# A decoder layer on one core: the first block of a seven-product matmul evicted in another order, its difference operands made later

## The chip, the cores and the metric

The kernel runs on one core of a Trainium2 chip. The metric is the device time of one execution in microseconds (us). Engines are named as in the profile: PE is TensorE (matmuls; PEld its weight loads), DVE is VectorE, ACT is ScalarE, POOL is GpSimd, SP is SyncE, which issues most of the DMAs.

## The reference, cut to what matters

One layer of a decoder trunk, for one batch of 512 tokens with model width 1024, all in float32:

```
h  = RMSNorm(x);  z = h @ W_in
A  = retention(z);  Bt = dilated windowed attention(z)
x  = x + (sig(g_A) * (A @ W_A) + sig(g_B) * (Bt @ W_B)) @ W_o
x  = x + relu(RMSNorm(x) @ W_up)^2 @ W_down          # W_down is 4096 x 1024
x  = x + sig(RMSNorm(x) @ W_pg) * (p @ W_pp)
```

The change touches the two steps `... @ W_o` and `... @ W_down`, and the very start of the kernel.

## The kernel before

Every large matmul is done in three: each operand is split into a high part (rounded to the matmul's float32r type) and a low part (the rest), and high x high, high x low and low x high are added up in PSUM (`mm3`, lines 246 to 251). So each weight block must be split on its way. A weight block of 128 x 1024 per partition row set is called a unit. `make_plan` lists all units in the order in which they are used. `fetch` (line 187) issues a unit's load from SP into one of six `raw` buffers, for some units with a second, adding DMA from POOL (L202) into the same buffer. `ahead` (line 205) runs the split of a unit: ACT rounds `raw` into `whi` (L237), DVE subtracts into `wlo` (L238), each in one of four buffers. `units(n)` (line 217) is called by a gemm for its next units; it has all units up to `AHEAD` further ones split, so AHEAD sets how early in the program the splits stand.

**The seven-product matmul.** `@ W_o` and each 1024-row part of `@ W_down` is a 2 x 2 block matmul in Strassen's way: seven products of combined blocks in place of eight. `seven_gemm` (line 1001) does it, five times in the kernel: first for W_o (in `tail`, line 1099), then four times for W_down (line 1149). The left operands were combined and split before (`seven_left`). The right operands are sums or differences of weight blocks. `plan_seven` (line 164) plans 14 units for it, two halves of the inner dimension for each product. Numbered from 0, in the order of use: units 0 to 5 are products 4, 3, 5 for the first half and again for the second; 6 and 7 are product 2; 8 and 9 product 1; 10 and 11 product 7; 12 and 13 product 6. Units 8 and 9 load nothing: each is a difference of blocks that are already in `raw` buffers, those of units 6 and 2, and of units 7 and 5. `ahead` makes both differences in place on DVE (L215) right behind the split of unit 7. They free the raw buffers of units 2 and 5 for later loads.

One product with one half is 12 matmuls of 512 columns on PE, six for each of two token blocks p. Product 4 gathers in two banks of PSUM, 3 in two more, 5 in two; 2 is added later on top of 4's banks, 7 on 5's and 6 on 3's; product 1 has two banks of its own. Hence bank 4 must be copied out (`m4`, ACT, L1040) before product 2 starts. The results are added to the residual x by `acc` on DVE (L1026). The copies and the first accumulations stand behind the sixth product step, product 5 with half 1.

**What follows each finished part.** `done` calls `ready`, which puts a transpose of the finished part of x in a list with a lag in ticks (`gain_T`, line 358); a product step ticks once behind the matmuls of each p, and a tick issues one ripe item (`tick`, line 115). The item (`split_T`, line 318) is four PE transposes (L325), then the split of their result out of PSUM, on ACT (L338, `h2h` or `h3h`) and DVE (L339, `h2l` or `h3l`). For tokens 0 to 255, columns 512 to 1023, the lag is one tick, and the PSUM banks are those of product 1, which starts two product steps later. `ready` exists for the first of the five matmuls (it feeds the MLP) and for the last (it feeds the gate); the three between have none.

**What sets the order.** The tile framework's planner orders the instructions of each engine. For the first matmul and the last, the kernel puts ACT and DVE under `manual_schedule` (lines 1097 and 1146), so that these two engines keep the written order there; PE and the DMA queues don't. The three matmuls between are left to the planner. AHEAD is set to 3 for the first and the last; `seven_gemm` sets 2 before product 7, and so the three between run with 2.

**The start.** `setup` clears a tile `warm` (L406), has ACT touch one element of it (L407) and runs seven bfloat16 matmuls on it (L410) while the first data arrive. Those matmuls read 512 bfloat16 columns, which are the first 256 of the tile's 512 float32 columns.

Of the kernel before, what the change touches and what calls it, by code (L numbers as in the profile page):

```python
# [13 lines left out]
AF = mybir.ActivationFunctionType  # L14
ALU = mybir.AluOpType
# [57 lines left out]
def R(ap):  # L73
    return ap.bitcast(F32R)


class Block:
# [86 lines left out]
    def plan_seven(self, w, r0):  # L164


        q = lambda i, j, u: w[r0 + 512 * i + 256 * u : r0 + 512 * i + 256 * (u + 1), 512 * j : 512 * (j + 1)]
        n = len(self.plan)
        for u in range(2):
            self.plan.append(((q(1, 0, u), q(0, 0, u)), None))  # L170
            self.plan.append(((q(0, 1, u), q(1, 1, u)), None))
            self.plan.append((q(1, 1, u), None))
        for u in range(2):
            self.plan.append((q(0, 0, u), None))
        self.differences[n + 7] = [(n + 6 + u, n + 2 + 3 * u) for u in range(2)]
        for u in range(2):
            self.plan.append(((None, n + 6 + u, n + 2 + 3 * u), None))
        for u in range(2):
            self.plan.append(((q(1, 0, u), q(1, 1, u)), None))
        for u in range(2):  # L180
            self.plan.append(((q(0, 0, u), q(0, 1, u)), None))
# [23 lines left out]
    def ahead(self, n):  # L205
        while len(self.loaded) < min(len(self.plan), self.used + n):
            i = len(self.loaded)
            self.fetch(i + 1)
            raw, g0 = self.raws[i]
            src = self.plan[i][0]  # L210
            if isinstance(src, tuple) and src[0] is None:
                g0 = None
            self.loaded.append(self.split_unit(raw, g0))
            for v, w in self.differences.get(i, ()):
                self.nc.vector.tensor_tensor(self.raws[v][0], self.raws[v][0], self.raws[w][0], op=ALU.subtract)  # L215

    def units(self, n):
        self.ahead(n + (0 if self.pinned else self.AHEAD))
# [158 lines left out]
    def setup(self):  # L377
        nc, a = self.nc, self.a
        self.gcol = self.const.tile([P, 48], F32, name="gcol")
        xr = [self.big("xr") for _ in range(2)]  # L380
        self.x_cols = [xr[k // 4][:, k % 4] for k in range(KD)]
        nc.scalar.dma_start(self.gcol, a["vec_cols"])
        for u in range(KD // 2):
            src, _ = self.plan[u]
            raw = self.wraw.tile([P, 1024], F32, tag="raw", name=self.nm("raw")).rearrange("p (k n) -> p k n", k=2)
            for k in range(2):
                c = slice((2 * u + k) * P, (2 * u + k + 1) * P)
                first = u == 0 and k == 0
                x = lambda i: nc.sync.dma_start(self.x_cols[2 * u + k][:, i], a["x_cols"][c, i])
                x(slice(0, 256) if first else slice(0, S))  # L390
                nc.sync.dma_start(raw[:, k], src[k * P : (k + 1) * P])
                if first:
                    x(slice(256, S))
            self.raws.append((raw, None))
        self.load_tables()
        self.fetch(6)
        self.x_tiles = []
        xb = [self.big("x") for _ in range(2)]
        for t in range(NT):
            v = xb[t // 2].rearrange("p (t c) n -> p t (c n)", t=2)[:, t % 2]  # L400
            nc.sync.dma_start(v, a["x"][0, t * P : (t + 1) * P])
            self.x_tiles.append(v)
        self.ident = self.const.tile([P, P], F32, name="ident")
        make_identity(nc, self.ident)
        warm = self.tmp("warm")
        nc.vector.memset(warm, 0.0)  # L406
        nc.scalar.activation(warm[:, 500:501], warm[:, 501:502], AF.Copy)  # L407
        wb, wps = warm.bitcast(mybir.dt.bfloat16), self.bank("warm")
        for _ in range(WARM):
            nc.tensor.matmul(wps, wb[:, :P], wb[:, :512], start=True, stop=True)  # L410
        self.mhalf = self.const.tile([P, H], F32, name="mhalf")
        nc.gpsimd.memset(self.mhalf, -0.5)
# [588 lines left out]
    def seven_gemm(self, U, xs, f, ready):  # L1001


        nc = self.nc
        LEFT = {1: 3, 2: 4, 3: 0, 4: 6, 5: 1, 6: 5, 7: 2}
        banks = {}

        def product(m, bank, u, first, last):
            (wh, wl), = self.units(1)
            for p in range(2):  # L1010
                if first and m != 1:
                    banks[bank, p] = self.gbank() if m in (3, 4) else self.bank("pb")
                ps = banks[bank, p]
                for k in range(2):
                    kk = 2 * u + k
                    c = slice(LEFT[m] * 256 + p * P, LEFT[m] * 256 + (p + 1) * P)
                    sh, sl = (R(U[i][kk].rearrange("p a b -> p (a b)")[:, c]) for i in range(2))
                    self.mm3(ps, sh, sl, wh[:, k], wl[:, k], first and k == 0, last and k == 1, m != bank)
                self.tick()

        X = lambda i, j, p: xs[2 * i + p][:, 512 * j : 512 * (j + 1)]

        def acc(i, j, p, v, sign=0):
            t, x = 2 * i + p, X(i, j, p)
            c = sign * NT + t
            nc.vector.scalar_tensor_tensor(x, v, f[:, c : c + 1], x, op0=ALU.mult, op1=ALU.add)  # L1026

        def done(i, j, p):
            if ready is not None:
                ready(2 * i + p, j, banks.get((1, p)))  # L1030

        for u in range(2):
            for m in (4, 3, 5):
                product(m, m, u, u == 0, u == 1)
        m4 = []
        for p in range(2):
            banks[1, p] = self.bank("pb")
        for p in range(2):
            t = self.tmp("m4")
            nc.scalar.activation(t, banks[4, p], AF.Copy)  # L1040
            m4.append(t)
            acc(0, 1, p, banks[3, p])
            acc(0, 1, p, banks[5, p], 1)
            done(0, 1, p)
        for u in range(2):
            product(2, 4, u, False, u == 1)
        for p in range(2):
            acc(1, 0, p, banks[4, p])
            done(1, 0, p)
            acc(1, 1, p, banks[4, p], 1)  # L1050
        for u in range(2):
            product(1, 1, u, u == 0, u == 1)
        for p in range(2):
            nc.vector.tensor_tensor(m4[p], m4[p], banks[1, p], op=ALU.add)
            acc(0, 0, p, m4[p])
            acc(1, 1, p, m4[p])
        self.AHEAD = 2
        for u in range(2):
            product(7, 5, u, False, u == 1)
        for p in range(2):  # L1060
            acc(0, 0, p, banks[5, p])
            done(0, 0, p)
        for u in range(2):
            product(6, 3, u, False, u == 1)
        for p in range(2):
            acc(1, 1, p, banks[3, p])
            done(1, 1, p)
# [165 lines left out]
```

## Time and profile before

| | us |
|---|---|
| runs | 993.36, 993.45, 993.88 (median 993.45) |
| the profiled execution | 993.55 |
| its span, first to last instruction | 991.8 |
| PE busy / DVE / ACT / POOL | 984.9 / 648.8 / 462.1 / 98.1 |
| L215 on DVE, ten instructions, each | 1.22 |
| L237 on ACT, 128x1024, each | 1.06 |
| L238 on DVE, 128x1024, each | 1.22 |

The first of the five matmuls runs on PE from 558.2 us of the span, the last from 900.2. A row of a timeline is: start, length, engine, line, operation, output and inputs by the program's names, shapes, count; in brackets the idle time of the engine before it and what ended it. Rows of the chain of waits are start, length and what was running. Lengths of matmul rows are modelled and overlap the next matmul; their starts are what counts. A row of busy times by window is: the window, its length, busy time, count, the clock granted to PE, the busy share of the DMA engines, GB/s.

### The profile page before, as it was taken

Reading aid. Unit: us, or ns where it says so; the run is one execution under the profiler, and the core shown is the slowest. Engines: PE = TensorE matmul, PEld = TensorE weight load, DVE = VectorE, ACT = ScalarE, POOL = GpSimd, SP = SyncE. Lnnn points to the kernel's source line nnn. Section 1 sums busy time; section 2 is a strip of 40 time slices with the busy share of each in tenths; the row PEclk is TensorE's granted clock in tenths of the full one; section 3 lists DMA queues with packets and bytes.
Section 4 is the critical chain, followed back from the end, with each engine's and each line's share of the span. In section 5 each row is a group of like instructions: output and inputs, shape, how many; then the busy total and the mean of one; then the engine's idle time right before and its main releaser. Section 6 shows DMA issues by size and latency. Waiting matters only on the chain.

```text
span 991.8 us, 12456 instructions
## 1 busy us (share of the span) xinstructions
PE 984.9 (99%) x4588; PEld 826.7 (83%) x4588; DVE 648.8 (65%) x1015; ACT 462.1 (47%) x939; POOL 98.1 (10%) x98
## 2 busy tenths in 40 slices
PE   9999999999999999999999999999999999999998
PEld 6888899889888888888888888888888888888886
DVE  7858675774869345454733796678667769767953
ACT  6635344433334334243423448664563565465451
POOL 0310120220000010001002000100101001000000
PEclk9999999999999999999999999999999999999999
DMA  9723122333234322222446486758749767875911
GB/s 333 262 85 87 44 85 85 113 98 98 83 109 153 124 63 76 96 65 86 162 135 156 137 218 201 185 141 221 184 132 226 187 159 170 228 174 128 298 54 54
DMA packets 90910, 141.16 MB, mean 142 GB/s; under 512 B 6320, under 2 KB 40672, under 8 KB 90848
## 3 DMA queue, kind: packets, MB, share of 16 engines
q1 hardware_dynamic: 79824, 119.36, 37.3%
q0 software_dynamic: 10880, 20.97, 12.6%
q8 instruction: 36, 0.59, 0.2%
q14 instruction: 26, 0.21, 0.1%
q10 hardware_dynamic: 144, 0.02, 0.0%
HBM read 136.10 MB, written 4.24 MB: 141 GB/s over the span
## 4 chain that ended last, share of the span: by engine, by line
PE 97%; DVE 1%; ACT 1%; DMA 1%; SPq 0%; issue 0%; ACTq 0%; DVEq 0%
PE pg L249 27%; PE pg L251 27%; PE pg L250 27%; PE pb L251 3%; PE pb L250 3%; PE pb L249 3%; PE po L699 1%; PE ph L555 1%; PE pt L325 1%; PE sc L676 1%; PE ry L905 1%; PE pe L647 1%; PE kv L893 1%; PE sc L682 1%; PE ry L907 1%; DMA raw<-in_w_in 1%
## 5 line engine op out<-in xcount | busy, mean ns | idle before, releaser
L238 DVE TENSOR_TENSOR wlo<-raw,whi 128x1024 fp32r<-128x1024 f32 (+1 forms) x166 | 196.8, 1190 | 104.3 <-ACT whi L237 102.4
L237 ACT ACTIVATE whi<-raw 128x1024 fp32r<-128x1024 f32 (+1 forms) x165 | 169.7, 1033 | 194.9 <-PE pg L251 71.5
L249 PE MATMUL pg<-whi,hh 128*128 128x512 f32 x440 | 177.3, 403 | 0.0
L251 PE MATMUL pg<-whi,hl 128*128 128x512 f32 x440 | 172.2, 391 | 0.0
L250 PE MATMUL pg<-wlo,hh 128*128 128x512 f32 x440 | 171.9, 391 | 0.0
L251 PEld LDWEIGHTS pg<-whi,hl 128*128 128x128 f32 x440 | 90.4, 206 | 15.1
L249 PEld LDWEIGHTS pg<-whi,hh 128*128 128x128 f32 x440 | 90.5, 206 | 13.8
L250 PEld LDWEIGHTS pg<-wlo,hh 128*128 128x128 f32 x440 | 90.7, 206 | 13.6
L249 PE MATMUL pg<-h2h,whi 128*128 128x512 f32 x256 | 99.6, 389 | 0.0
L250 PE MATMUL pg<-h2l,whi 128*128 128x512 f32 x256 | 99.6, 389 | 0.0
L251 PE MATMUL pg<-h2h,wlo 128*128 128x512 f32 x256 | 99.6, 389 | 0.0
L242 ACT ACTIVATE whi<-raw,gcol 128x256 fp32r<-128x256 f32 (+1 forms) x144 | 66.2, 525 | 22.1 <-PE pg L250 12.4
L243 DVE SCALAR_TENSOR_TENSOR wlo<-raw,gcol,whi 128x256 fp32r<-128x256 f32 (+1 forms) x144 | 65.6, 511 | 15.6 <-ACT whi L242 15.6
L202 POOL DMA_DIRECT2D raw<-in_w_down x32 | 38.6, 1206 | 302.8 <-DMA raw<-in_w_down 188.2
L249 PE MATMUL pg<-hh,whi 128*128 128x512 f32 x160 | 64.0, 400 | 0.0
L249 PE MATMUL pg<-whi,uh 128*128 128x512 f32 x160 | 62.8, 393 | 0.1
L251 PE MATMUL pg<-whi,ul 128*128 128x512 f32 x160 | 62.5, 392 | 0.0
L250 PE MATMUL pg<-wlo,uh 128*128 128x512 f32 x160 | 62.5, 391 | 0.0
L251 PE MATMUL pg<-hh,wlo 128*128 128x512 f32 x160 | 62.4, 390 | 0.0
L250 PE MATMUL pg<-hl,whi 128*128 128x512 f32 x160 | 62.3, 389 | 0.0
L250 PEld LDWEIGHTS pg<-h2l,whi 128*128 128x128 f32 x256 | 48.1, 188 | 10.0
L249 PEld LDWEIGHTS pg<-h2h,whi 128*128 128x128 f32 x256 | 48.1, 188 | 9.9
(201 smaller groups left out, 1693.2 us busy)
## 6 DMA issues: line engine op xcount, KB each, us to landing
raw<-in_w_in SPq DMA_DIRECT2D x72, 512.0 KB, 3.9
raw<-in_w_down SPq DMA_DIRECT2D x48, 512.0 KB, 4.3
raw<-in_w_up SPq DMA_DIRECT2D x32, 512.0 KB, 4.8
raw<-in_w_down POOLq DMA_DIRECT2D x32, 512.0 KB, 6.7
raw<-in_w_o SPq DMA_DIRECT2D x12, 512.0 KB, 3.9
x<-in_x SPq DMA_DIRECT2D x8, 512.0 KB, 6.9
raw<-in_w_ret_out SPq DMA_DIRECT2D x8, 512.0 KB, 3.5
raw<-in_w_o POOLq DMA_DIRECT2D x8, 512.0 KB, 5.8
```

The source lines that it names most:

```text
L202: self.nc.gpsimd.dma_start(raw, rows(add[0]), accum_op=ALU.add)
L237: self.pin(nc.scalar.activation(R(hi[:, i]), raw[:, i], AF.Copy))
L238: nc.vector.tensor_tensor(R(lo[:, i]), raw[:, i], hi[:, i], op=ALU.subtract)
L242: self.pin(nc.scalar.activation(R(hi[:, i]), raw[:, i], AF.Copy, scale=g))
L243: nc.vector.scalar_tensor_tensor(R(lo[:, i]), raw[:, i], g, hi[:, i], op0=ALU.mult, op1=ALU.subtract)
L249: t.matmul(ps, sh, mh, start=first, stop=False, skip_group_check=more)
L250: t.matmul(ps, sh, ml, start=False, stop=False, skip_group_check=more)
L251: t.matmul(ps, sl, mh, start=False, stop=last, skip_group_check=more)
L325: nc.tensor.transpose(ps[:, k * P : (k + 1) * P], part[:, k * P : (k + 1) * P], self.ident)
L555: self.nc.tensor.transpose(ps[:, t * P : (t + 1) * P], rots[t][:, h * HD : (h + 1) * HD], self.ident)
L647: self.nc.tensor.transpose(ps[:, k * P : (k + 1) * P], e[:, k * P : (k + 1) * P], self.ident)
L676: nc.tensor.matmul(sc[:, h * P : (h + 1) * P], qT[:, h, rs], kT[:, h, rs], start=True, stop=True)
```

## The change

Three edits.

1. The differences for units 8 and 9 are no longer both made behind the split of unit 7. Each is made directly ahead of the split of its own unit.
2. In `seven_gemm` the order of the matmuls stays 4, 3, 5, 4, 3, 5. The copies of bank 4 are now written behind product 4's second half, the accumulations of banks 3 behind product 3's second half; those of banks 5 stay behind product 5's second half. AHEAD is 2 for the call of product 5's second half, and is then set to 3 until `seven_gemm` sets 2 before product 7 as it did. This holds for all five matmuls, also the three that had run with 2 throughout.
3. Half of the tile `warm` is cleared, the half that the warm-up matmuls read, and ACT touches an element in that half.

```
@@ plan_seven
-        self.differences[n + 7] = [(n + 6 + u, n + 2 + 3 * u) for u in range(2)]
         for u in range(2):
+            self.differences[n + 8 + u] = n + 6 + u, n + 2 + 3 * u
             self.plan.append(((None, n + 6 + u, n + 2 + 3 * u), None))
@@ ahead
+            if i in self.differences:
+                v, w = (self.raws[k][0] for k in self.differences[i])
+                self.nc.vector.tensor_tensor(v, v, w, op=ALU.subtract)
             self.loaded.append(self.split_unit(raw, g0))
-            for v, w in self.differences.get(i, ()):
-                self.nc.vector.tensor_tensor(self.raws[v][0], self.raws[v][0], self.raws[w][0], op=ALU.subtract)
@@ setup
-        nc.vector.memset(warm, 0.0)
-        nc.scalar.activation(warm[:, 500:501], warm[:, 501:502], AF.Copy)
+        nc.vector.memset(warm[:, :256], 0.0)
+        nc.scalar.activation(warm[:, 250:251], warm[:, 251:252], AF.Copy)
@@ seven_gemm
-        for u in range(2):
-            for m in (4, 3, 5):
-                product(m, m, u, u == 0, u == 1)
-        m4 = []
+        for m in (4, 3, 5):
+            product(m, m, 0, True, False)
+        m4 = [self.tmp("m4") for _ in range(2)]
+        product(4, 4, 1, False, True)
+        for p in range(2):
+            nc.scalar.activation(m4[p], banks[4, p], AF.Copy)
+        product(3, 3, 1, False, True)
+        for p in range(2):
+            acc(0, 1, p, banks[3, p])
+        self.AHEAD = 2
+        product(5, 5, 1, False, True)
         for p in range(2):
             banks[1, p] = self.bank("pb")
         for p in range(2):
-            t = self.tmp("m4")
-            nc.scalar.activation(t, banks[4, p], AF.Copy)
-            m4.append(t)
-            acc(0, 1, p, banks[3, p])
             acc(0, 1, p, banks[5, p], 1)
             done(0, 1, p)
+        self.AHEAD = 3
```

## The prediction

> **What bounds the kernel now.** I read the page first, then the chain of work that ended last, then the timelines of the engines around the places where that chain leaves TensorE.
>
> ```profile
> span 991.8 us, 12456 instructions
> PE 984.9 (99%) x4588; PEld 826.7 (83%) x4588; DVE 648.8 (65%) x1015; ACT 462.1 (47%) x939; POOL 98.1 (10%) x98
> PE 97%; DVE 1%; ACT 1%; DMA 1%; SPq 0%; issue 0%; ACTq 0%; DVEq 0%
> ```
>
> TensorE carries 97% of the chain; 991.8 - 984.9 = 6.9 us is all that it stands idle. The change alters no matmul, so it can only remove a part of that idle time, or add to it. Between the start and the last few us of the kernel, the long pieces of the chain that are not TensorE's stand in two places only, and both lie in the two products that run with a fixed order on ACT and DVE: the first (w_o) and the last (the fourth w_down). I write P5.1 for product 5 with half 1 (the halves are 0 and 1), and unit 8 for the first difference unit. The first place, in the chain view (start, length, what):
>
> ```profile
> 569.86 1.07 ACT whi L237
> 570.96 1.23 DVE wlo L238
> 572.18 1.14 DVE raw L215
> 573.43 1.06 ACT whi L237
> 574.49 0.49 ACT m L1040
> 575.02 0.50 PE pg L249
> ```
>
> Unit 7 is split, the subtract of L215 runs, unit 8 is split, and only then does ACT copy bank 4 (L1040), for which P2.0 waits at 575.02. The second place, in the timelines of DVE, ACT and PE around the last product:
>
> ```profile
> 913.47 2.35 DVE L215 TENSOR_TENSOR raw<-raw,raw 128x1024 f32<-128x1024 f32 x2
> 915.90 1.23 DVE L238 TENSOR_TENSOR wlo<-raw,whi 128x1024 fp32r<-128x1024 f32 x1
> ...
> 918.26 0.75 DVE L1026 SCALAR_TENSOR_TENSOR x<-pb,f,x 128x512 f32<-128x512 f32 x1 [0.47 <-DVE x L1026]
> 918.92 0.74 DVE L1026 SCALAR_TENSOR_TENSOR x<-pg,f,x 128x512 f32<-128x512 f32 x1
> 919.77 0.75 DVE L1026 SCALAR_TENSOR_TENSOR x<-pb,f,x 128x512 f32<-128x512 f32 x1
> 920.44 1.22 DVE L238 TENSOR_TENSOR wlo<-raw,whi 128x1024 fp32r<-128x1024 f32 x1
> 921.57 1.28 DVE L339 TENSOR_TENSOR h3l<-pb,h3h 128x512 fp32r<-128x512 f32 x2
> ```
>
> ```profile
> 914.80 1.06 ACT L237 ACTIVATE whi<-raw 128x1024 fp32r<-128x1024 f32 x1 [2.51 <-DVE raw L215]
> 915.77 1.06 ACT L1040 ACTIVATE m<-pg 128x512 f32<-128x512 f32 x2
> 916.72 1.06 ACT L237 ACTIVATE whi<-raw 128x1024 fp32r<-128x1024 f32 x1
> 919.76 0.60 ACT L338 ACTIVATE h3h<-pb 128x512 fp32r<-128x512 f32 x1 [1.98 <-PE pb L325]
> ```
>
> ```profile
> 916.24 0.39 PE L251 MATMUL pb<-whi,ul 128*128 128x512 f32 x1
> ...
> 918.35 0.39 PE L251 MATMUL pg<-whi,ul 128*128 128x512 f32 x1
> 919.06 0.66 PE L325 MATMUL pb<-ident,x 128*128 128x128 f32 x4 [0.33 <-DVE x L1026]
> ...
> 923.22 0.39 PE L251 MATMUL pg<-whi,ul 128*128 128x512 f32 x1
> 923.44 0.39 PE L249 MATMUL pb<-whi,uh 128*128 128x512 f32 x1
> ```
>
> 916.24 is the last matmul of P5.1; the four transposes at 919.06 wait for the accumulation of 918.26; 923.44 is the first matmul of P1.0. Two things to see. ACT stood idle for 2.51 us before 914.80, waiting for the subtract, although the bank that its next instruction copies had long been full: in this region ACT and DVE keep the written order, even when that means waiting. And matmuls follow each other by 0.23 us (923.22 to 923.44, from P2.1 into P1.0 without a wait), so without the wait the transposes would have started at about 918.58: the stall is 0.48 us.
>
> The same two matmuls, the last of P5.1 and the first of P1.0, in the first product:
>
> ```profile
> 574.57 0.39 PE L251 MATMUL pb<-whi,ul 128*128 128x512 f32 x1
> ...
> 581.72 0.39 PE L249 MATMUL pb<-whi,uh 128*128 128x512 f32 x1
> ```
>
> P2.0 would start 0.23 behind 574.57, at 574.80; the copy holds it until 575.02, 0.22 us.
>
> **What the change removes.** The copies of bank 4 and the accumulations of banks 3 move ahead, before P5.1 ends. Both stalls go: 0.48 and 0.22 us, with the transposes' smaller wait in the first product perhaps 0.8 us in all. ACT's copies now precede the split of unit 7, which comes some 0.5 us later; P2.1 needs it more than 5 us after, so that costs nothing.
>
> **What it adds.** AHEAD is 2 in the call of P5.1, so no new unit is split there, and 3 again in the call of P2.0, which then brings two units, 8 and 9, each now as subtract, whi, wlo. This is issued before the first transposes of P2.0 are evicted (they are queued with a lag of one tick, and the tick comes after the matmuls). So the written order on DVE becomes: last accumulation of bank 5, subtract 8, wlo 8, subtract 9, wlo 9, then h3l of the two transposed tiles; on ACT: whi 8, whi 9, h3h, h3h. Behind each subtract stands a whi on the other engine, and behind that a wlo: a chain with no overlap. Its length, from rows:
> - subtract to whi: 914.80 - 913.47 = 1.33.
> - whi 8, wlo 8, subtract 9, whi 9: the chain view has exactly this ring, 573.43 - 569.86 = 3.57.
> - whi to wlo: 570.96 - 569.86 = 1.10.
> - wlo to the next DVE instruction: 921.57 - 920.44 = 1.13.
> Together 7.13 us from subtract 8 to the start of the first h3l. Before, only one wlo (1.13) stood there, with its whi long done.
>
> Who waits for it: the transposes of P2.0 go into the banks of product 1 (the rows say pb), so P1.0 cannot start writing until h3l has read the first one. One h3l, from the view by tile:
>
> ```profile
> L339 DVE TENSOR_TENSOR h3l<-pb,h3h x2: 681/682/684, 921.6 to 922.2; 128x512 fp32r<-128x512 f32 x2
> ```
>
> Last product: P5.1 ends at 916.24 + 0.39 = 916.63; an engine starts 0.04 behind what it waits for (919.06 + 0.66 = 919.72, ACT at 919.76); the last accumulation takes 0.66 to the next one's start (918.92 - 918.26); subtract 8 starts at 917.33, h3l at 924.46, ends 0.68 later, and P1.0 starts at 925.18. Before it started at 923.44: **+1.74 us**, the removed stall already in it. TensorE arrives at about 922.96, so it would stand for 2.2 us.
> First product, the same steps from 574.57: end 574.96, subtract 8 at 575.66, h2l at 582.79, done at 583.47, P1.0 at 583.51 against 581.72: **+1.79 us**.
>
> **What comes behind.** DVE is the later engine from there on:
>
> ```profile
> 921.57:936.81 15.24, 15.10 (x22) 1.00 1.07 328
> ```
>
> ```profile
> 935.40 1.41 DVE L1026 SCALAR_TENSOR_TENSOR x<-pb,f,x 128x512 f32<-128x512 f32 x2
> ```
>
> ```profile
> 936.64 0.60 PE L325 MATMUL pt<-ident,x 128*128 128x128 f32 x4
> ```
>
> In the stretch of the first row (length, DVE busy) DVE works 15.10 of 15.24 us, so it makes nothing up. It is 924.46 - 921.57 = 2.89 late, TensorE 1.74. The next thing that TensorE takes from DVE in the critical sense is x, added at 935.40 and done about 0.75 later, transposed at 936.64: 0.45 us of slack, against 1.15 of extra lateness. That is up to 0.7 us more in each of the two products; the transposes can also stand a few matmuls later in TensorE's order, which is not fixed, and then cost nothing. I take 0.3 each, **+0.6 us**, ends 0 and 1.4.
>
> **The DMAs behind the subtracts.** The subtract frees the buffers for the loads of units 12 and 13:
>
> ```profile
> 914.71 1.55 SPq L200 DMA_DIRECT2D raw<-in_w_down  x2
> ```
>
> ```profile
> raw<-in_w_down SPq DMA_DIRECT2D x48, 512.0 KB, 4.3
> ...
> raw<-in_w_down POOLq DMA_DIRECT2D x32, 512.0 KB, 6.7
> ```
>
> SP issues both as the subtracts end. In the last product subtract 9 now ends at 917.33 + 3.57 + 1.22 = 922.1; load 4.3 and the adding DMA on POOL 6.7 give 933.1, some 934 with the hand-over. The first use is P6.1, which began behind the 936.64 row and will begin near 939; whi and wlo take 2.3. So there are 2 to 3 us of room and I take 0; if the loads that SP issues behind it slow it, up to 1 us in each product. Those loads are moved too, but their units are used later still.
>
> **The three products between** (planner's order, not the written one):
>
> ```profile
> 669.21 1.22 DVE L215 TENSOR_TENSOR raw<-raw,raw 128x1024 f32<-128x1024 f32 x1
> ```
>
> ```profile
> 772.41 0.48 PE L250 MATMUL pg<-wlo,uh 128*128 128x512 f32 x1
> 772.73 0.39 PE L251 MATMUL pg<-whi,ul 128*128 128x512 f32 x1
> ```
>
> There the planner already sets a subtract between two accumulations, and no transposes use product 1's banks. The only trace of pressure is 772.41, in P6.1 of the third product, which is 0.09 us longer than its neighbours. Written later, the subtract may fall behind one or more accumulations of 0.66 us; if unit 13 comes later by that in all three, 2.0 us. I take 0: nothing is removed there, and a planner that fills idle DVE time has the same holes. At most 0.1 us could be gained.
>
> **The warm-up tile.**
>
> ```profile
> 0.92 0.48 DVE L406 MEMSET warm<- 128x512 f32 x1 [0.92 <-PEq L1211]
> 4.17 0.43 DVE L233 CAST whi<-raw 128x512 fp32r<-128x512 f32 x1 [2.76 <-DMA raw<-in_w_in]
> ```
>
> Half the memset saves about 0.24 us of DVE and lets the warm-up start that much earlier. But DVE then waits 2.76 us for a DMA that this doesn't touch, and the first real matmul waits for that cast: 0.
>
> **Sum.** 1.74 + 1.79 + 0.6 = +4.1 us. The profiled execution took 993.55 us (991.8 of span and 1.75 around it), so 997.7; the median of the runs shown, 993.45, is 0.10 under it: **997.6 us**.
>
> **Rivals.**
> A, not slower: the evictions of the transposes pass the two splits, because the planner, or the order of the ticks, sets them earlier than I read it. Then the old stalls go and nothing comes: 993.45 - 0.9 = 992.6 us. It decides at the first h3l: started before 922.2 on the old scale, P1.0 does not wait. For it: ACT's and DVE's whole work is small (65% and 47%). Against it: ACT's 2.51 us of obedient idling. Chance 0.15. The change not doing what it says is the same case in part: were the two units split as before, P2.0 would only lose its stall.
> B, half of it: only one of the two products meets the wait, or some of the chain of 7.13 overlaps. About +1.9, so 995.3. Chance 0.10.
> C, more comes with it: the DMAs of unit 13 or the three middle products cost 1 to 3 us on top, 999 to 1001. The slack is thin in the middle (772.41). Chance 0.10.
> D, the clock. A standstill of 2.2 us of TensorE is longer than the stalls above (0.48 and 0.22), and the granted clock (the 1.00 of the DVE window row) is full. At the kernel's start TensorE is slower:
>
> ```profile
> 1.46 3.17 PE L410 MATMUL warm<-warm 128*128 128x512 bf16 x7 [1.46 <-DVE warm L406]
> ```
>
> Seven matmuls in 3.17 us, over 0.4 us each against 0.23 later, though of another type. If TensorE fell back to that pace behind each standstill for as long as this row lasts, it would lose nearly half of 3.17, some 1.5 us, twice: 3 us more, 1000.6. The Trainium skill, "TensorE: Matmul & The Clock Gate", section "Why this matters for your kernels", warns of gaps over about 3 us between bursts of matmuls; by that the 2.2 us would just pass, and the sum would stay as it is. No row of before shows a gap of that length. Chance 0.03.
> The forecast itself has 0.62.
>
> **How the numbers follow.** A measurement of this kernel can tell about 0.2% from no change, 2.0 us. The forecast with its own ends, 996.9 (nothing behind the two waits, 993.45 + 3.53 - 0.1 in the middle products) to 999.4 (1.4 behind them and 1 from the DMAs), is slower by over that bound; so are C and D; B lies at the bound, half to each side. Slower: 0.62 + 0.10 + 0.03 + 0.05 = 0.80, cut to 0.78. A is within the bound, and with half of B makes 0.20. Faster by 2.0 us would need more than the removable stalls of under 1 us: 0.02. The range takes in the forecast, half of B, and the lower part of C and D: 995.2 to 999.8.
>
> **What would show it.** In the profile after: L1040 on ACT ahead of the split of unit 7; L215 twice as single instructions with whi and wlo between them, behind the last L1026 of bank 5; the first h2l and h3l some 7 us behind the first subtract; TensorE idle by about 2 us before the first pb matmul of P1.0, at about 583.5 and, counted on the shifted scale, 927; the transposes before it without a wait; the start and the middle products as before. The prediction is wrong if the h3l rows come before the second L215, if TensorE's idle time in those two places is under 1 us, or if the time falls.

## The result, and the profile after

| | before | after |
|---|---|---|
| median of the runs, us | 993.45 (993.16 to 993.98, six) | 1000.0 (999.25 to 1000.81, six) |
| the profiled execution | 993.55 | 999.74 |
| its span | 991.8 | 997.9 |

The ratio is 1.0065, 95% interval 1.0052 to 1.0078: slower by 6.55 us where the forecast was 4.1 slower, and just beyond the end of its range (999.8). Three executions of the runs below, of 1234.86 to 3554.03 us, were slow throughout and are in no median and no range.

From the page of the changed kernel:

```profile
span 997.9 us, 12446 instructions
PE 985.9 (99%) x4588; PEld 828.5 (83%) x4588; DVE 648.1 (65%) x1015; ACT 461.0 (46%) x939; POOL 98.0 (10%) x98
PE 98%; DVE 1%; ACT 1%; issue 0%; ACTq 0%
```

These totals hide the change: TensorE's busy time is 1.0 us longer with the same 4588 matmuls, DVE's work is the same. The span, 6.1 us longer, has to be found in places. Its chain of waits in the first product (lines of the changed file are up to 5 higher):

```profile
576.45 1.14 DVE raw L215
577.70 1.07 ACT whi L238
578.79 1.23 DVE wlo L239
580.02 1.15 DVE raw L215
581.27 1.07 ACT whi L238
582.36 1.01 DVE wlo L239
```

This is the ring of the prediction, twice around, without any overlap. The timeline of DVE in the last product has the same ring ahead of the eviction, and that of TensorE shows who waits:

```profile
921.52 1.22 DVE L215 TENSOR_TENSOR raw<-raw,raw 128x1024 f32<-128x1024 f32 x1
923.94 1.23 DVE L239 TENSOR_TENSOR wlo<-raw,whi 128x1024 fp32r<-128x1024 f32 x1 [1.21 <-ACT whi L238]
925.09 1.22 DVE L215 TENSOR_TENSOR raw<-raw,raw 128x1024 f32<-128x1024 f32 x1
927.51 1.22 DVE L239 TENSOR_TENSOR wlo<-raw,whi 128x1024 fp32r<-128x1024 f32 x1 [1.21 <-ACT whi L238]
928.65 1.28 DVE L340 TENSOR_TENSOR h3l<-pb,h3h 128x512 fp32r<-128x512 f32 x2
```

```profile
581.65 0.39 PE L252 MATMUL pg<-whi,ul 128*128 128x512 f32 x1
584.24 0.79 PE L250 MATMUL pb<-whi,uh 128*128 128x512 f32 x1 [2.19 <-DVE h2l L340]
584.83 0.63 PE L251 MATMUL pb<-wlo,uh 128*128 128x512 f32 x1
...
926.80 0.39 PE L252 MATMUL pg<-whi,ul 128*128 128x512 f32 x1
929.39 0.50 PE L250 MATMUL pb<-whi,uh 128*128 128x512 f32 x1 [2.20 <-DVE h3l L340]
929.73 0.39 PE L251 MATMUL pb<-wlo,uh 128*128 128x512 f32 x1
```

Subtract 8 to h3l is 928.65 - 921.52 = 7.13 us, the ring's sum to the hundredth. P1.0 starts 584.24 - 581.65 - 0.23 = 2.36 us late, and in the last product 929.39 - 926.80 - 0.23 = 2.36 us. But the two stops are not alike behind their first matmul: 584.24 to 584.83 is 0.59 us, 929.39 to 929.73 is 0.34. The clock tells why, by busy times in windows of 1 us (the number behind the count is the granted clock):

```profile
584.00:585.00 1.00, 0.76 (x2) 0.63 0.81 297
585.00:586.00 1.00, 1.00 (x4) 0.50 0.78 168
...
587.00:588.00 1.00, 1.00 (x5) 0.66 1.14 260
...
929.00:930.00 1.00, 0.61 (x3) 1.00 0.89 254
930.00:931.00 1.00, 1.00 (x6) 1.00 0.74 170
```

Behind the first stop TensorE had half its clock. A share of 0.63 is 0.74 us at half, so it fell at 584.26; 0.66 is 0.68 us at half, so it rose at 587.68: 3.42 us at half, in which 1.71 us of work are lost. Behind the second stop nothing fell.

The other new place is the start. Timelines of TensorE, ACT and DVE:

```profile
2.73 3.15 PE L411 MATMUL warm<-warm 128*128 128x512 bf16 x7 [2.73 <-ACT warm L408]
5.31 2.25 PE L465 MATMUL pg<-whi,hh 128*128 128x512 f32 x4
```

```profile
1.18 1.28 ACT L408 ACT_TABLE_LOAD   x1 [1.18 <-PEq L1216]
2.47 0.20 ACT L408 ACTIVATE warm<-warm 128x1 f32<-128x1 f32 x1
```

```profile
0.86 0.27 DVE L407 MEMSET warm<- 128x256 f32 x1 [0.86 <-PEq L1216]
```

The half memset is 0.21 us shorter, close to the 0.24 forecast. But the warm-up matmuls now start at 2.73 rather than 1.46, and the bracket names ACT: the element that ACT touches lies in the half that they read, so they wait for its touch, which stands behind a table load of 1.28 us. Before, it lay in the half that they don't read. The cast that the first real matmul was to wait for is done at 4.87 (a DVE row from 4.44, 0.43 long), and the matmul starts at 5.31 with no wait in brackets, right behind the warm-up: it is the warm-up that holds it now.

Following each matmul's start from kernel to kernel, in us later than before, and what each stretch adds:

| place | after minus before | step |
|---|---|---|
| when the start is over | 0.70 | +0.70 |
| first matmul of P1.0, first product | 2.52 | +1.82 |
| behind the slow stretch | 4.27 | +1.75 |
| ahead of the last product | 4.18 | -0.1 |
| first matmul of P1.0, last product | 5.95 | +1.77 |
| end of the span | 6.1 | +0.15 |

The steps at P1.0 are the stop of 2.36 us less the old stalls, which are gone: just ahead of P1.0 the two kernels are 0.17 us apart in the first product and 3.59 in the last. The step of the start is one pair of executions; in two more profiles of the changed kernel, below, it is 0.88 and 0.35.

### The profile page after: what moved, and what is told of

It reads as the page before. It is cut to its first block, busy times and chain, and to the rows that moved or that the text cites. A ratio compares the mean times of both kernels' runs of the same rounds, so it can differ in the third digit from the quotient of the medians.

```text
span 997.9 us, 12446 instructions
## 1 busy us (share of the span) xinstructions
PE 985.9 (99%) x4588; PEld 828.5 (83%) x4588; DVE 648.1 (65%) x1015; ACT 461.0 (46%) x939; POOL 98.0 (10%) x98
## 4 chain that ended last, share of the span: by engine, by line
PE 98%; DVE 1%; ACT 1%; issue 0%; ACTq 0%
PE pg L250 27%; PE pg L252 27%; PE pg L251 26%; PE pb L250 3%; PE pb L251 3%; PE pb L252 3%; PE po L700 1%; PE ph L556 1%; PE pt L326 1%; PE sc L677 1%; PE ry L906 1%; PE pe L648 1%; PE kv L894 1%; PE sc L683 1%; PE ry L908 1%; DVE raw L215 0%
## 5 line engine op out<-in xcount | busy, mean ns | idle before, releaser
L252 PEld LDWEIGHTS pg<-h2h,wlo 128*128 128x128 f32 x256 | 48.0, 188 | 9.9
```

The costliest lines, as they stand in the source:

```text
L252: t.matmul(ps, sl, mh, start=False, stop=last, skip_group_check=more)
```

## The experiments

T1 in the expectations is the theory that the two stops come from the ring ahead of the evictions, the rest from the late warm-up and the clock. A time without an interval beside it is the median of its runs; the kernel before had 993.46 to 993.54 beside these.

**The warm-up alone**: edit 3 put into the kernel before.

```
-        nc.vector.memset(warm, 0.0)
-        nc.scalar.activation(warm[:, 500:501], warm[:, 501:502], AF.Copy)
+        nc.vector.memset(warm[:, :256], 0.0)
+        nc.scalar.activation(warm[:, 250:251], warm[:, 251:252], AF.Copy)
```

> The kernel before with the third edit alone: half of the warm-up tile cleared, ACT's touched element moved into that half. Theory 1, the touched element is now among those that the warm-up matmuls read, so they wait for ACT's first instruction, which stands behind the loading of its table: the warm-up starts at about 2.7 us of the span in place of 1.46, PE reaches its full pace about 1.2 us later, and the whole is 0.7 us slower (994.1). Rival, the later start is an accident of the one profiled execution: warm-up at about 1.2, time as before (993.4).

994.22 us (993.77 to 994.49), ratio 1.0007 [0.9998, 1.0016]: 0.76 us by the medians, which the interval doesn't quite part from nothing. So it was profiled once more:

> The kernel before with the third edit alone, for a profile of it. Theory (the warm-up matmuls wait for ACT's touch, because the touched element now lies in what they read): first L410 matmul at about 2.7 us instead of 1.46, first L463 or L464 matmul 0.5 to 0.7 us later than in the kernel before, about 994.2 us. Rival (the late warm-up comes only with the other edits): first warm-up matmul at 1.2 to 1.5 us, 993.4 us.

```profile
2.72 3.14 PE L410 MATMUL warm<-warm 128*128 128x512 bf16 x7 [2.72 <-ACT warm L407]
5.30 0.99 PE L464 MATMUL pg<-whi,hh 128*128 128x512 f32 x1
```

The same wait, the first real matmul 0.56 us later (5.30 against 4.74), and 994.25 us. Nothing else of the change is needed for it.

**Half the memset, the touch outside**:

```
-        nc.vector.memset(warm, 0.0)
+        nc.vector.memset(warm[:, :256], 0.0)
+        nc.vector.memset(warm[:, 500:502], 0.0)
```

> The kernel before with half of the warm-up tile cleared, but ACT's element left in the other half (its two elements are cleared by a memset of their own). Theory 1: the matmuls wait for the first memset alone, the warm-up starts at about 1.2 us, and the time is that of before or up to 0.2 us less (993.2 to 993.4). Rival, it is the halved memset that costs: 0.7 us slower, as the third edit alone.

993.37 us, ratio 0.9999 [0.9990, 1.0008]. Its warm-up starts at 1.19 us, released by the memset on DVE. The half memset itself is worth nothing that shows; where the touch lies is worth the 0.7.

**Edits 1 and 2 without 3**:

> The changed kernel with the third edit undone. Theory 1: the start is as before, the two stops of 2.36 us before the first matmul of product 1 stay, and so does the fall of the granted clock behind one or both; 0.7 us less than the changed kernel, about 999.3, and it varies by more than 1 us between executions with the place of the stop in the clock's window. Rival, the clock fell because of the late warm-up: no fall here, 993.45 + 3.6 = 997.1 with little spread.

1000.34 us (999.51 to 1000.92), ratio 1.0070 [1.0057, 1.0082]. The 0.7 us that should have been saved are not to be seen between these two kernels. The profiled execution, of 999.51 us, has both stops, with the clock fallen behind the first. So the clock falls without the late warm-up too. A fall takes 1.71 us of some 998, 0.0017, from the granted clock averaged over the span, and the record has this average for each execution. (The clock also falls in the last us of a span, which takes up to about as much again.) Three of the five show 0.996, which one fall can't make; one, of 1000.62 us, shows 1.000, so it had none. What moves single executions by 1.7 us and more covers 0.7 in a median of five.

**One unit at a time behind product 5**: as that, but AHEAD is set to 3 only after the call of P2.0, which so brings unit 8 alone.

```
-        self.AHEAD = 3
         for u in range(2):
             product(2, 4, u, False, u == 1)
+            self.AHEAD = 3
```

> The changed kernel with the third edit undone and AHEAD left at 2 for the call of P2.0, so that this call splits unit 8 alone and unit 9 comes with the call of P2.1, behind the evictions of the transposes. Theory 1: one round of subtract, whi, wlo (1.33 + 1.10 + 1.13 = 3.56 us) stands before the evictions in place of 7.13; they end some 1 us before PE needs the banks, the stops go, and with them the fall of the clock; the old stalls of before are gone too: 992.6 to 993.2. Rival, the stop comes from making the differences late at all: still a stop of over 1 us at product 1, 995 or more.

994.96 us (994.4 to 997.64), ratio 1.0018 [1.0009, 1.0028]: 1.8 us above the top of what was expected. The stops at P1.0 are gone; another is there. TensorE, ACT and the chain near it, in the profiled execution of 997.64 us, the longest of the ten:

```profile
598.89 0.50 PE L251 MATMUL pg<-wlo,uh 128*128 128x512 f32 x1 [2.00 <-DVE wlo L239]
```

```profile
590.69 1.06 ACT L238 ACTIVATE whi<-raw 128x1024 fp32r<-128x1024 f32 x1 [2.26 <-DMA raw<-in_w_o]
```

```profile
582.01 8.59 DMA raw<-in_w_o
```

P6.1 waits 2.0 us for a wlo, and behind this stop the clock falls too, at 599.82. The chain leads back to unit 12, whose load was issued behind subtract 8 and whose adding DMA took 8.59 us rather than the median of 6.7 that the prediction used. ACT waits 2.26 us for it, and DVE, in written order, has unit 12's wlo, an eviction and six additions ahead of unit 13's wlo. So the term "DMAs behind the subtracts", set to 0, is not 0 as soon as the stop ahead of it is gone. The other nine executions show a granted clock of 0.999 or 1.000, so no fall, and took 994.4 to 996.17 us all the same.

**Both subtracts back behind unit 7**: the run with edits 1 and 2 with edit 1 undone, so the early copies, accumulations and AHEAD of edit 2 alone. The core of it:

```
-            if i in self.differences:
-                v, w = (self.raws[k][0] for k in self.differences[i])
-                self.nc.vector.tensor_tensor(v, v, w, op=ALU.subtract)
             self.loaded.append(self.split_unit(raw, g0))
+            for v, w in self.differences.get(i, ()):
+                self.nc.vector.tensor_tensor(self.raws[v][0], self.raws[v][0], self.raws[w][0], op=ALU.subtract)
```

> The changed kernel with edits 1 and 3 undone: both subtracts stand behind the split of unit 7 again; the earlier copies and accumulations and the AHEAD values of the change stay. T1 (the stops before P1.0 come from the subtracts standing in one ring with two splits ahead of the h2l and h3l evictions): without the subtracts the ring of 7.13 us shrinks to two splits, whose whi can follow each other, so the 2.36 us stops at P1.0 go or fall under 0.7 us each, no clock fall, 992.8 to 994.2. Rival (it is enough that P2.0's call brings two units, whatever they hold): stops of over 1.2 us stay at P1.0 in both products, 996 to 999. Second rival (as in the run with one unit): the loads behind the subtracts come later and P6.1 stops instead, 994.5 to 997.

992.43 us (991.85 to 992.67), ratio 0.9987 [0.9978, 0.9996]: faster than the kernel before by 1.0 us, than the run with edits 1 and 2 by 7.9, and a little below the range expected. P2.0 still brings two units, in the timeline of DVE (last product), and TensorE doesn't stop:

```profile
918.00 2.35 DVE L238 TENSOR_TENSOR wlo<-raw,whi 128x1024 fp32r<-128x1024 f32 x2
920.27 1.28 DVE L339 TENSOR_TENSOR h3l<-pb,h3h 128x512 fp32r<-128x512 f32 x2
```

```profile
917.66 0.60 PE L325 MATMUL pb<-ident,x 128*128 128x128 f32 x4
```

Without subtracts between them both whi are done early, two wlo cost 2.27 us instead of 7.13, and the h3l starts 1.30 us ahead of its place before the change (921.57); 0.86 of that this execution had gained ahead of the last product. The transposes at 917.66 have no wait: the old stall is gone too. It is the place of the subtracts that costs, not the number of units; T1 holds, the rival falls.

**Subtracts in the gaps**: the kernel before with the early copies and accumulations, subtract 8 behind the split of unit 6, subtract 9 between the two accumulations of banks 5, AHEAD as before. The core of it:

```
+        def difference(u):
+            v, w = self.raws[n + 6 + u][0], self.raws[n + 2 + 3 * u][0]
+            nc.vector.tensor_tensor(v, v, w, op=ALU.subtract)
...
+        self.ahead(3)
+        difference(0)
+        product(3, 3, 1, False, True)
...
         for p in range(2):
             acc(0, 1, p, banks[5, p], 1)
             done(0, 1, p)
+            if p == 0:
+                difference(1)
```

> The kernel before, with the copies of bank 4 and the accumulations of banks 3 ahead as in the change, but subtract 8 right behind the split of P4.1's call, subtract 9 between the two accumulations of banks 5, and AHEAD, plan and warm-up as before. T1: no ring ahead of the evictions, early loads of units 12 and 13, the old stalls of 0.48 and 0.22 us gone: 992.3 to 993.2, no stop of over 0.5 us in the first and last product. Rival (the order is a closed balance: a subtract between the accumulations delays done() and the transposes by 1.2 us, and PE waits there instead): 993.5 to 995.5.

992.5 us, ratio 0.9987 [0.9978, 0.9996]. A second way to the same 1 us, so that is what the old stalls were worth.

**How long a stop must be.** Spare additions on DVE in the kernel before, ahead of P2.0's call in the first and the last product:

```
+        if ready is not None:
+            spare = self.tmp("spare")
+            for _ in range(4):          # and 7
+                nc.vector.tensor_tensor(spare, X(1, 1, 0), X(1, 1, 0), op=ALU.add)
```

> The kernel before with four spare DVE additions of 128x512 (about 0.66 us each, 2.6 us in sum, of which about 1.2 us are slack) ahead of P2.0's call in the first and the last product; the output is the same, the additions feed nothing. A probe of the clock: a stop of about 1.4 to 1.8 us at P1.0 in both products. Theory (a stop costs more than itself only when it is long enough for the clock to fall): no fall behind these, 996.2 to 997.3, spread of the runs under 1 us. Rival (any stop of over 1 us can bring a fall, by its place in time): some runs 1.7 or 3.5 us longer, median 998 to 1000.5, matmuls 0.43 us apart behind a stop.

995.8 us (994.78 to 996.55). TensorE stood still twice for 1.19 and 1.17 us, less than expected; 993.5 + 2.4 = 995.9, so the stops cost their own length. The clock stayed at 1.00 behind them, and its average is 0.999 or 1.000 in all ten executions: no fall in any.

> As the probe with four additions, but with seven (about 4.6 us in sum): stops of about 3.4 to 3.9 us at P1.0 in both products. Theory (the clock falls behind a stop that is long enough): matmuls 0.43 us apart for about 3.4 us behind both stops, 1.75 us lost at each, 993.45 + 7.2 + 3.5 = 1003.5 to 1004.8, narrow spread. Rival (the clock's fall does not depend on the length of the stop): a fall behind one or none, 1000.2 to 1002.6.

1004.39 us (1001.64 to 1004.71); two stops of 3.36 us make 993.5 + 6.7 = 1000.2, and 4.2 are left for the clock. Its windows:

```profile
584.00:585.00 1.00, 0.00 (x0) 0.76 1.12 205
...
590.00:591.00 1.00, 1.00 (x3) 0.50 0.49 172
591.00:592.00 1.00, 1.00 (x6) 0.82 0.00 0
...
932.00:933.00 1.00, 0.00 (x0) 0.84 1.02 186
...
936.00:937.00 1.00, 1.00 (x6) 0.95 0.82 281
```

By the working above the clock fell at 584.52 and rose at 591.36, 6.84 us, twice 3.42; it fell at 932.68 and rose at 936.10, 3.42. TensorE worked in 5.6 and in 3.0 of these us, half of which is 4.3. The narrow spread that was expected is missing: the execution of 1001.64 us shows an average clock of 0.998, against 0.994 and 0.995 in the other three, so a stop of this length doesn't always bring the whole loss.

**The changed kernel, profiled twice more**:

> The changed kernel, profiled a second time. Theory (granted clock falls for some 3.4 us when a stop of 2.36 us happens to fill enough of a fixed window of the clock's control, and the windows do not start with the program): a time of 997.7 with no fall, 999.4 with one, 1001.2 with two, and the falls seen in the profile number what the time says; first fall possible at any offset behind 584. Rival (the clock is the same in each execution, one fall at the first stop and none at the second, and the spread has another source): one fall at 584.24 again, whatever the time.

1001.46 us, and two falls; windows:

```profile
584.00:585.00 1.00, 0.55 (x2) 0.87 0.85 305
...
929.00:930.00 1.00, 0.44 (x1) 0.75 0.71 229
```

> The changed kernel, profiled a third time; the same expectations as for the second profile: time minus 997.7 over 1.75 gives the number of falls seen, 0, 1 or 2, against one fall at 584.24 each time.

999.92 us, and one fall, behind the second stop this time, none behind the first:

```profile
584.00:585.00 1.00, 1.00 (x5) 1.00 0.70 213
...
928.00:929.00 1.00, 1.00 (x3) 0.67 0.55 141
```

Four falls at six stops, and in these three the number of falls goes with the time: 999.74 and 999.92 with one, 1001.46 with two. The rival, the same fall in each execution, is out. But falls aren't all that moves the time: of the six timed executions those of 999.25 and 1000.74 us show an average clock of 0.999, which leaves no room for a fall, the other four 0.997 or 0.998. The one of 1000.74 had no fall and is as long as others with one or two. What it waited for isn't on record.

**The stops filled.** Edits 1 and 2 again, with nine matmuls of zeros in the gap, added to an open bank of product 2 (`zero` is a bfloat16 tile of 512 columns, cleared at the start):

```
+        if ready is not None:
+            for _ in range(9):
+                nc.tensor.matmul(banks[4, 1], self.zero[:, :P], self.zero, start=False, stop=False, skip_group_check=True)
```

> The changed kernel with edit 3 undone, as the run with edits 1 and 2, plus nine matmuls of zeros (bfloat16, 512 columns, added to an open bank, so that nothing changes) behind product 2 in the first and the last product: they fill about 2.0 of the 2.36 us in which TensorE stands still ahead of P1.0, and delay nothing. Theory (the stops cost their own length, and the clock's fall behind them costs 1.75 us each on top): P1.0 as late as without them, but no matmuls 0.43 us apart behind it; 997.0 to 997.6, with up to 0.9 more for a late unit 13 at P6.1 that the falls had hidden; no run above 998.8. Rival (the slow stretch behind the stop comes from something else, such as the DMAs in flight then, or the time above 997 is elsewhere): slow matmuls behind P1.0 all the same, 999.5 to 1001.

999.06 us (997.79 to 999.52), ratio 1.0057 [1.0043, 1.0070]. The execution profiled was the one of 997.79:

```profile
581.63 1.89 PE L1056 MATMUL pg<-zero 128*128 128x512 bf16 x8
583.76 0.50 PE L250 MATMUL pb<-whi,uh 128*128 128x512 f32 x1 [0.24 <-DVE h2l L340]
584.10 0.40 PE L251 MATMUL pb<-wlo,uh 128*128 128x512 f32 x1
```

P1.0 still starts when the h2l lets it, and the clock stays at 1.00 behind it. That is what the theory asked for; the executions up to 999.52 are not, it had none above 998.8. Three more profiles:

> The run with the filled stops, profiled again, because its executions spread from 997.79 to 999.52 and the one profiled was the shortest. Theory (what is over 997.8 is a wait of P6.1 for a late unit 13, with or without a fall of the clock behind it): an execution above 998.5 shows a gap of 0.5 to 2.5 us on TensorE at P6.1, near 599 or 940, and matmuls 0.43 us apart behind it if the gap is over 2. Rival (clock falls behind P1.0 although the stop is filled): slow matmuls directly behind 583.8 or 927.3.

> As the profile before it: a gap at P6.1 near 599 or 940 for an execution above 998.5, against slow matmuls directly behind P1.0.

> As the two profiles before it: a gap at P6.1 near 599 or 940 for an execution above 998.5, against slow matmuls directly behind P1.0.

999.41, 998.82 and 997.74 us, and no fall of the clock in any. TensorE in the longest, and then the same instruction of ACT, unit 12's whi, in the execution of 997.79 and in the longest:

```profile
599.33 0.50 PE L251 MATMUL pg<-wlo,uh 128*128 128x512 f32 x1 [0.70 <-DVE wlo L239]
...
943.46 0.66 PE L326 MATMUL pt<-ident,x 128*128 128x128 f32 x4 [0.77 <-DVE x L1029]
```

```profile
590.05 1.06 ACT L238 ACTIVATE whi<-raw 128x1024 fp32r<-128x1024 f32 x1 [1.48 <-DMA raw<-in_w_o]
```

```profile
591.12 1.06 ACT L238 ACTIVATE whi<-raw 128x1024 fp32r<-128x1024 f32 x1 [2.79 <-DMA raw<-in_w_o]
```

In P6.1 of both products TensorE stands still, for 0.86 and 0.93 us; in the first product unit 12's DMA lands 1.07 us later (ACT waits 2.79 us for it, not 1.48, and starts at 591.12, not 590.05), and DVE's written order hands that on. The one of 998.82 has one such gap, of 0.43, a little under the 0.5 expected, and its start took 0.7 us longer; the one of 997.74 has one, of 0.57. So these transfers, whose landing moves from one execution to the next, cost 0 to 1.8 us in these four executions, in which no fall of the clock hides them.

## Why the prediction was wrong

The sum put three terms at nothing that were not nothing: the start, the clock behind the two stops, and in some executions the transfers behind the subtracts. The stops themselves it had right.

**The two stops: right.** "+1.74" and "+1.79" measured 1.77 and 1.82, by the ring of 7.13 us, with P1.0 waiting for the first h2l or h3l. Putting the subtracts back behind unit 7 (992.43 us against 1000.34) shows their place to be the cause. Rivals A and B are out: every profile of the changed kernel has both stops.

**The warm-up tile: the step failed.** "The first real matmul waits for that cast: 0" measured +0.70. I priced the shorter memset and took ACT's touch to be as far from the warm-up matmuls as before. It had become a writer of what they read: a wait added, with 1.28 us of table load ahead of it. So the first real matmul waits for the warm-up and no longer for the cast. The Trainium skill, "ScalarE: Activation LUTs", section "What ACT_TABLE_LOAD costs", gives such a load about 1283 ns; the trace agrees (1.28).

**The clock, rival D: the step that cost most, given 0.03 and nothing in the sum.** Its price was nearly right ("some 1.5 us" per stop; 1.75 measured), its chance was not. It rested on two things. No row of before showed a stop of that length, which bounds nothing. And the Trainium skill, "TensorE: Matmul & The Clock Gate", warns in its section "Why this matters for your kernels" of gaps of over 3 us, and its section "What's actually happening" has the clock fall after at least one idle window of 3413 ns. Here it fell behind stops of 2.36 us, four times in six, and the measurement decides. Of D's two falls the changed kernel's three profiles have one, two and one. Filling the gap took the falls away with P1.0 just as late (none at eight stops, against five at eight in the four profiles with the gaps open), so the standstill is the cause.

**"What comes behind": +0.6** measured 0.1 to 0.2 in the profiled execution. The lateness of DVE that it named is there; the row of 943.46 above is its very place, with 0.93 us. It costs nothing where the clock has made TensorE later still.

**The DMAs behind the subtracts: 0** in the profiled execution, up to 1.8 us together with the term before it where the stops were filled, 2.0 at P6.1 with one unit at a time. "If the loads that SP issues behind it slow it, up to 1 us in each product" had the right size, but unit 12 led, not unit 13. In the third profile of the changed kernel, where the first stop brought no fall, P6.1 of the first product stood still for 0.45 us. Rival C, whose range (999 to 1001) holds the measured median, asked for 1 to 3 us from these transfers or the middle products; no profile of the changed kernel shows that, but the execution of 1000.74 without a fall leaves it open for some. **The middle products: 0** measured -0.1.

**The sum.** 993.45 + 0.70 + 1.82 + 1.77 + 0.1 = 997.8, next to the 997.6 forecast: without the clock the forecast would have looked right, its 0.6 too much behind the stops making up for the 0.7 missed at the start; that would have been luck. Each fall adds 1.75: 999.6 with one, 1001.3 with two, against 999.74, 999.92 and 1001.46 in the three profiles. That the first of these sums lands near the median of 1000.0 is in part luck: by their average clock two of the six timed executions had no fall, and one of these two, 1000.74, is 2.9 us above 997.8 by something that isn't shown.

## What to carry to other kernels

Count what stands in written order ahead of an eviction that frees a PSUM bank: operations that alternate between two engines cost their sum there (7.13 us here), while the subtracts made earlier cost nothing. A stop of TensorE of over 2 us is to be priced at its length plus a possible fall of the clock (1.75 us here), and a delay that is removed in one place may only uncover a late transfer behind it. When a touched element, a slice or a memset moves, list anew who reads and writes what: that is where waits are added unseen.

## What the runs showed of the hardware

The falls fit fixed windows. In the run with seven additions the two falls are 932.68 - 584.52 = 348.16 us apart, and every stretch at half clock behind a stop is 3.42 us long or twice that: 348.16 is 102 steps of 3.4133. The second profile of the changed kernel fits: its falls, at 584.74 and 929.50, are 344.76 apart, 101 steps. The Trainium skill, "TensorE: Matmul & The Clock Gate", section "What's actually happening", has a free-running window of 3413 ns; these agree. If the windows lie so that one ends at each fall, the share of the window in which TensorE had worked can be worked out: behind the first stop of the changed kernel the window is 580.85 to 584.26, the stop 581.88 to 584.24, so it worked in 1.05 of 3.41 us, 31%. In the executions where one stop brought a fall and the other did not, the other's window follows by steps of 3.4133.

| stop | worked in the window | fall |
|---|---|---|
| changed kernel, first profile: first, second | 31%, 42% | yes, no |
| second profile: first, second | 31%, 33% | yes, yes |
| third profile: first, second | 39%, 31% | no, yes |
| edits 1 and 2: first, second | 31%, 41% | yes, no |
| one unit at a time, P6.1 | 37% | yes |
| seven additions: first, second | 37%, 13% | yes, yes |

All falls lie at 37% or less, the three stops without one at 39% or more. That is a reading of eleven stops, not a test of its own. The two stops of the run with four additions agree with it: by steps from the one fall that its profile shows, at 992.33 in the last us, their windows are worked in by 73% and 66%, and neither brought a fall. By this reading, as an estimate, a stop of under 2.1 us can't bring a fall, and one of 2.36 can or can't as it meets the windows. In the run with seven the window behind the first fall was worked in by 64% and the clock stayed at half; windows worked in by 88% and more brought it back.
